# Sums of the down weights made in DRAM, and lower parts of mixer weights split in place: one decoder layer on one core

## The chip, the cores and the metric

The kernel runs on one core of a Trainium2 chip. The core has TensorE (PE, matrix products), VectorE (DVE), ScalarE (ACT), GpSimd (POOL) and SyncE (SP, here a queue that issues transfers); 16 DMA engines move data between DRAM and the on-chip memory (SBUF). The metric is the time of one execution in microseconds (us); lower is better.

## The reference

One layer over 512 tokens of width 1024, in float32:

```python
x = x + 0.5 * rms_norm(swiglu(rms_norm(x, g1), w_gate1, w_up1, w_down1), p1)
x = x + rms_norm(hybrid_mixer(rms_norm(x, g2), w_in, ...), p2)
x = x + 0.5 * rms_norm(swiglu(rms_norm(x, g3), w_gate2, w_up2, w_down2), p3)

def swiglu(h, w_gate, w_up, w_down):          # 1024 -> 2816 -> 1024
    return (silu(h @ w_gate) * (h @ w_up)) @ w_down
```

The mixer projects with `w_in`, runs four heads of differential attention and eight heads of a sparse attention with three branches, and projects back with `w_out`.

## The kernel before

**Two parts of each operand.** TensorE works on float32r, so each float32 operand is split in an upper part (a cast) and a lower part (the value less the upper part). A product takes three matmuls: upper by upper, upper by lower, lower by upper. The function `split` makes both parts: the cast on ACT or DVE (line 404), the subtraction on DVE (line 407). A loaded weight piece is 128 x 1024 float32, 512 KB; it lands in a tile of the pool `raw` (four of them), and its two parts go to the pool `ring` (twelve).

**Seven products in place of eight.** The gate, up and most of the down products are done with the Strassen-Winograd scheme: a 2 x 2 block product with seven block products (numbered 1 to 7) and sums of blocks. For the down weights, `down_products` cuts rows 768 to 2815 of `w_down` in two row halves `kh` and two column halves `jh`; each such block is cut in four quarter rows `q`, so that a piece is again 512 KB. `ORDER` = (1, 5, 6, 2, 7, 4, 3) is the order of the products. Products 1, 2 and 3 take a block as it is. Product 5 takes block (0,0) + block (0,1); product 6 adds block (1,1) to that; product 4 adds block (1,0) to the sum of 6; product 7 takes block (0,1) + block (1,1). `factor` loads the quarters and DVE adds them (line 601), for products 5, 6 and 4 in place in the tiles `ff1du` or `ff2du`, 16 additions in each block. Then `split` makes `ff1dw53h` and `ff1dw53l`: product 5, quarter row 3, upper and lower part. The left operands are `ff1dl`. Line 808 is the matmul of these products. The other 768 rows are done plainly (line 768).

**Lower parts of mixer weights prepared ahead.** For three groups of 512 columns of `w_in` (four pieces each) `ahead` loads a piece during the first feed-forward block (`pre`), casts it on ACT (line 352), subtracts on DVE (line 353) and stores the lower part to DRAM (`low`, line 354). In the mixer `piece` loads the piece anew, makes the upper part (line 377), and loads the lower part from DRAM straight into the ring (line 380, `wp26l` to `wp37l`).

**Norms.** `prenorm` and `postnorm` square on ACT (line 447), and POOL makes the reciprocal root (`rstd`, lines 439 and 440), on which DVE's scaling waits. The normalised tile is transposed on PE and becomes the right operands `xa` (first block), `xb` (mixer), `xc` (second block).

**The order.** Every step is an operation in a graph with a planned cost, its data and its buffers. `Graph.order` plans all engines by list scheduling: the operation with the largest level, the longest path to the end plus a term from the table `BIAS`, goes first as soon as its data and a buffer are there. The program is emitted in that order; each engine then runs its own instructions in that order and waits on semaphores for the others. SP issues nearly all transfers, also in order. A list of edges (`after`) holds back some operations in the plan.

Of the kernel before, what the change touches and what calls it, by code (L numbers as in the profile page):

```python
# [18 lines left out]
P = 128  # L19
# [34 lines left out]
    "ACT:fh>fdl": 5.6, "ACT:fh>fdl@ACT": -68.3, "ACT:fh>fdl@DVE": -0.3, "ACT:fh>fhh": 16.2, "ACT:fh>fhh@DVE": -182,
    "ACT:fhr>fhh": -138.7, "ACT:fhr>fhh@ACT": 20, "ACT:fhr>fhh@DVE": -242.2, "ACT:fp_>fp_": 134.6,
    "ACT:fqu>fqw": 937.3, "ACT:fqv>fqw": 100.3, "ACT:fy>fdp": 44, "ACT:gr>gh": 1255.8, "ACT:htk>hTk": -17.2,
    "ACT:htv>hTv": -173.1, "ACT:k__t>kT": 25.7, "ACT:ls>ls": 40.7, "ACT:n_nm>n_l": 46.2, "ACT:n_t>n_th": 116.1,
    "ACT:n_t>xa": -94.5, "ACT:n_t>xaf0": -210.9, "ACT:n_t>xaf1": 11.9, "ACT:n_t>xb": 327.4, "ACT:n_t>xc": 49.3,
    "ACT:n_t>xcf1": -137.4, "ACT:nc_pc>nc_pc": -84.3, "ACT:nc_t>nc_h": 25.6, "ACT:oN>oTn": 59.7,
    "ACT:oN>oTn@ACT": -12.7, "ACT:oN>oTn@DVE": -5.8, "ACT:pa>cd": 32.4, "ACT:pa>k__dup": 127.2, "ACT:pa>v": -109.4,  # L60
    "ACT:pb>k__dup": 21.1, "ACT:pb>v": 19.9, "ACT:pk>dkd": -48.9, "ACT:pre>pre": 191.7, "ACT:pre>preh": 0.9,
    "ACT:pv>dv": -90.4, "ACT:qTd_>qTd": 7.3, "ACT:qTn_>qTn": -44.2, "ACT:qd>qdd": 5.5, "ACT:qn>qdn": 23.6,
    "ACT:raw>wp": -2.3, "ACT:raw>wp@ACT": 20.1, "ACT:raw>wp@DVE": -4, "ACT:rawff1d>fdwh": 18.3,
    "ACT:rawff1d>fdwh@ACT": -113.1, "ACT:rawff1d>fdwh@DVE": -13.4, "ACT:rawff1q>fqw": 3.5, "ACT:rawff2d>fdwh": -25.9,
    "ACT:rawff2d>fdwh@ACT": -55.9, "ACT:rawff2d>fdwh@DVE": -67.9, "ACT:rawff2q>fqw": -83.9, "ACT:uk>uk": -98.6,
    "ACT:uv>uv": -22.7, "ACT:wrk>wk": 42.2, "ACT:wrv>wv": -96.2, "ACT:xaf0>xa": 12.9, "ACT:xaf0>xa@ACT": -0.2,
    "ACT:xaf0>xa@DVE": -99.7, "ACT:xaf1>xa": 5.7, "ACT:xaf1>xa@ACT": -49.8, "ACT:xaf1>xa@DVE": 21.3,
    "ACT:xcf0>xc": -165.4, "ACT:xcf0>xc@ACT": -92.6, "ACT:xcf1>xc": -156.2, "ACT:xcf1>xc@DVE": 213.5,
    "ACT:xi>n_ss": -6, "ACT:xj>n_ss": -11.3, "ACT:xm>n_ss": 95.1, "ACT:xrv>Xv": 189.3, "ACT:xrv>Xv@ACT": -72.1,
    "ACT:xrv>Xv@DVE": -45, "ACT:z>o_ss": 13.3, "DVE:acc>oN": -6, "DVE:cd_t>kc": 8, "DVE:ck>kcT": -19,  # L70
    "DVE:cmask>cmb": -77, "DVE:cmk>uk": -91.8, "DVE:cmv>uv": 103.6, "DVE:cv>vc": -15, "DVE:d>d_p": -21.7,
    "DVE:d_acc>o": 29.2, "DVE:d_r>d_p": 40.3, "DVE:d_t>d_th": 53.2, "DVE:dkt>dk": 7.8, "DVE:dl>d_r": -29.5,
    "DVE:dl>do_r": -0.4, "DVE:dmask>dmb": 5.2, "DVE:do_rr>o": 39.5, "DVE:do_t>oTd": 3.5, "DVE:fb>fhs": -65.9,
    "DVE:fb>fp_": 8.2, "DVE:fc>fhs": 24.7, "DVE:fc>fp_": 0.5, "DVE:fc__sg>fh": 23.8, "DVE:fd>fhs": -37.7,
    "DVE:fdp>fy": 12, "DVE:fdq>fy": 19.9, "DVE:fdr>fy": 1.9, "DVE:fds>fdl": 1.5, "DVE:fdu>fdwl": 62.2,
    "DVE:fh>fdl": -29.3, "DVE:fh>fds": 14.2, "DVE:fh>fh": 11.2, "DVE:fh>fhl": 92.5, "DVE:fh>fhl@DVE": 9.3,
    "DVE:fh>fhl@POOL": 1.1, "DVE:fhr>fhl": 156.6, "DVE:fp_>fh": 53.9, "DVE:fp_>fhs": 43.6, "DVE:fp_>fp_": 39.7,
    "DVE:fqu>fqw": 1255.3, "DVE:fqv>fqw": -218.6, "DVE:fy>fdr": 4.2, "DVE:gr>gh": 1080.8, "DVE:gsub>gsub": -24.1,
    "DVE:htk>hTk": -33.2, "DVE:htv>hTv": -60.3, "DVE:k__t>kT": 46.9, "DVE:lp>ls": 49, "DVE:ls>nlam": 0.6,
    "DVE:n>n_p": 4.9, "DVE:n_cf>n_p": 22, "DVE:n_cf>n_p@DVE": -1.2, "DVE:n_cf>n_p@POOL": 14, "DVE:n_l>n_cf": -8.8,  # L80
    "DVE:n_t>n_th": -9.5, "DVE:n_t>xa": -96.2, "DVE:n_t>xb": 0.5, "DVE:n_t>xc": 1861.1, "DVE:nc>nc_pc": -160.3,
    "DVE:nc_t>nc_h": -18.1, "DVE:oN>oTn@DVE": 0.7, "DVE:o_yg>xi": 22.6, "DVE:o_yg>xm": -74.8, "DVE:o_yg>xo": 136.3,
    "DVE:pa>k__dup": -42.2, "DVE:pb>k__dup": 6.6, "DVE:pb>v": 5.1, "DVE:pek>xrk": 235.1, "DVE:pev>xrv": 8.5,
# [11 lines left out]
    "PE:dkd>dk": -91, "PE:fdl>fy": 29.8, "PE:fqw>fa": 45.6, "PE:fqw>fb": -9.4, "PE:fqw>fc": 11096.3, "PE:gh>g_": 819,
    "PE:k__dup>kT": -118.5, "PE:n_p>n_th": 301.1, "PE:n_th>acc": 901.3, "PE:n_xn>n_t": 76.4, "PE:n_xn>xb": 123.4,
    "PE:n_xn>xc": -1.5, "PE:nc_h>acc": -5.5, "PE:nc_pc>nc_h": 103.1, "PE:o>oTd": 3.3, "PE:qTd>d_p": 30.9,
    "PE:qTn>n_p": -8.1, "PE:qTn>nc": 92.9, "PE:qdd>qTd": 32.2, "PE:qdn>qTn": -22.2, "PE:uk>hTk": 71.3,
    "PE:uv>hTv": 32.4, "PE:warm>warm": 23.6, "PE:wk>ck": -115.9, "PE:wp>cd": 543, "PE:wp>dkd": -66.7,
# [5 lines left out]
    "SP:g_mix_norm_post>g_mix_norm_post": 1.3, "SP:g_mix_norm_pre>g_mix_norm_pre": 52, "SP:gr>gr": 118.4,
    "SP:lamt>lamt": 110.2, "SP:low>wp": -30.4, "SP:pre>low": -83.8, "SP:pre>pre": 52.2, "SP:raw>raw": -2024,
    "SP:rawff1d>rawff1d": 312.4, "SP:rawff1q>rawff1q": 455.3, "SP:rawff2d>rawff2d": -5.8, "SP:rawff2q>rawff2q": 238.4,
    "SP:trig>trig": 3.2, "SP:wrk>wrk": -5.4, "SP:x>xm": 90.4, "SP:x>xo": -11, "SP:xi>xi": 427.6, "SP:xj>x": -7.4,
    "SP:xj>xj": 6.2, "SP:xm>x": -6.1, "SP:xm>xm": -3.5, "SP:xo>xo": -8.8,
# [1443 lines left out]
```

## Time and profile before

| | |
|---|---|
| median of 3 runs | 1001.36 us (1000.78 to 1003.04) |
| profiled execution | 1003.56 us, of which the span from first to last instruction is 1001.8 us |
| PE, DVE, ACT, POOL busy in the span | 983.5, 882.9, 589.5, 32.3 us |
| granted TensorE clock, mean | 0.995 of full speed (2.4 GHz) |
| moved by the hardware queue | 153.30 MB, 45.4% of 16 DMA engines' span |

A busy engine is one that runs an instruction; waits and the issuing of transfers do not count. The span runs from the first instruction to the last, the time of the execution has a little more around it. The first block's gate and up stage runs to about 242 us, its down stage to 350, the mixer to 658, the second block to the end.

### The profile page before, as it was taken

What the parts mean: (1) busy time and instruction counts of PE and PEld (TensorE: products, weight loads), DVE (VectorE), ACT (ScalarE), POOL (GpSimd) and SP (SyncE); (2) the same over time, 40 slices, a digit from 0 to 9 for tenths busy, and PEclk for the clock granted to TensorE, in tenths of its full rate; (3) what the DMA queues carried; (4) which work ended last, traced back from release to release, by engine and by line L of the source; (5) the groups of instructions that cost most, each with busy time, mean ns of one, the idle gap of its engine ahead of it and who ended that gap; (6) DMA issues with size and microseconds to landing.
All of it is one profiled execution on the core that took longest, in us unless ns stands there. A gap on an engine that the chain in (4) does not pass through costs nothing.

```text
span 1001.8 us, 17153 instructions
## 1 busy us (share of the span) xinstructions
PE 983.5 (98%) x6504; PEld 893.9 (89%) x6504; DVE 882.9 (88%) x1612; ACT 589.5 (59%) x1143; POOL 32.3 (3%) x68
## 2 busy tenths in 40 slices
...
GB/s 336 64 86 179 168 178 127 164 173 242 258 222 293 244 179 147 190 168 1 169 1 110 59 167 86 106 232 53 137 106 135 68 136 43 86 281 244 231 210 84
DMA packets 100420, 154.39 MB, mean 154 GB/s; under 512 B 11121, under 2 KB 61553, under 8 KB 100338
## 3 DMA queue, kind: packets, MB, share of 16 engines
q1 hardware_dynamic: 100338, 153.30, 45.4%
...
## 4 chain that ended last, share of the span: by engine, by line
PE 85%; DVE 6%; DMA 4%; ACT 2%; issue 1%; SPq 0%; POOL 0%; DVEq 0%; POOLq 0%; ACTq 0%
PE ff2b L664 9%; PE ff1b L664 9%; PE ff1y L808 7%; PE ff2c L664 6%; PE ff1c L664 6%; PE ff2a L664 6%; PE ff1a L664 6%; PE ff2y L808 5%; PE z L1410 4%; PE ff2y L768 3%; PE ff1y L768 2%; PE n_t L1306 2%; DMA rawff2d<-ff_w_down 1%; PE n L1190 1%; PE acc L398 1%
## 5 line engine op out<-in xcount | busy, mean ns | idle before, releaser
L1203 ACT ACTIVATE n_p<-n_p,n_nm 128x128 f32<-128x128 f32 (+3 forms) x64 | 35.3, 554 | 9.0 <-DVE n_nm L1201 8.6
L1201 DVE CUSTOM_DVE_ANT_0 n_p<-n,dmb 128x128 f32<-128x128 f32 (+3 forms) x64 | 28.3, 486 | 5.9 <-PE n L1191 5.6
L407 DVE TENSOR_TENSOR n_th<-n_t,n_th 128x512 fp32r<-128x512 f32 x40 | 25.8, 684 | 6.6 <-ACT n_th L404 6.4
L404 ACT CAST n_th<-n_t 128x512 fp32r<-128x512 f32 x40 | 21.6, 594 | 7.0 <-PE n_t L1306 6.7
L439 POOL TENSOR_SCALAR o_ms<-o_ss 128x1 f32<-128x1 f32 x12 | 4.0, 335 | 664.6 <-ACT junk L447 664.5
L691 ACT ACTIVATE ff1p<-ff1p 128x256 f32<-128x256 f32 x30 | 12.5, 418 | 19.2 <-DVE ff1p L703 19.2
L691 ACT ACTIVATE ff2p<-ff2p 128x256 f32<-128x256 f32 x30 | 12.5, 417 | 16.5 <-DVE ff2p L703 15.7
L1203 ACT ACTIVATE d_p<-d_p,d_nm 128x128 f32<-128x128 f32 (+3 forms) x32 | 17.7, 556 | 5.7 <-DVE d_nm L1201 5.5
L1306 PEld LDWEIGHTS n_t<-ident,n_p 128*128 128x128 f32 x160 | 18.6, 140 | 2.5
L1306 PE MATMUL n_t<-ident,n_p 128*128 128x128 f32 x160 | 20.7, 272 | 0.0
L703 DVE TENSOR_TENSOR ff2p<-ff2p,ff2b 128x512 f32<-128x512 f32 x30 | 20.4, 681 | 0.3 <-PE ff2b L664 0.3
L1190 PE MATMUL n<-kT,qTn 128*128 128x128 f32 (+3 forms) x64 | 20.4, 335 | 0.0
L703 DVE TENSOR_TENSOR ff1p<-ff1p,ff1b 128x512 f32<-128x512 f32 x30 | 20.4, 680 | 0.0
L1191 PE MATMUL n<-kT,qTn 128*128 128x128 f32 (+3 forms) x64 | 19.6, 321 | 0.0
L569 DVE TENSOR_TENSOR o_yg<-ff2y,g_ff_norm_post 128x512 f32<-128x512 f32 x8 | 5.5, 689 | 14.3 <-ACT junk L447 14.3
L447 ACT ACTIVATE junk<-ff2y 128x512 bf16<-128x512 f32 x8 | 4.8, 597 | 21.3 <-PE ff2y L768 21.3
L398 PE MATMUL acc<-n_th,v 128*64 128x512 f32 x40 | 16.1, 402 | 0.0
L1201 DVE CUSTOM_DVE_ANT_0 d_p<-d,dmb 128x128 f32<-128x128 f32 (+3 forms) x32 | 14.7, 486 | 1.2 <-PE d L1191 1.2
L399 PE MATMUL acc<-n_th,v 128*128 128x512 f32 x40 | 15.7, 393 | 0.0
L470 PE MATMUL n_t<-ident,n_xn 128*128 128x128 f32 x96 | 13.3, 286 | 1.2 <-DVE n_xn L463 1.2
L703 DVE TENSOR_TENSOR ff2p<-ff2c,ff2p 128x512 f32<-128x512 f32 x20 | 13.8, 688 | 0.3
L1296 DVE TENSOR_SCALAR n_p<-n_p,n_cf 128x128 f32<-128x128 f32 (+3 forms) x42 | 13.8, 380 | 0.3
...
## 6 DMA issues: line engine op xcount, KB each, us to landing
rawff1d<-ff_w_down SPq DMA_DIRECT2D x36, 512.0 KB, 4.7
rawff2d<-ff_w_down SPq DMA_DIRECT2D x36, 512.0 KB, 5.0
rawff1q<-ff_w_gate SPq DMA_DIRECT2D x22, 512.0 KB, 5.8
rawff1q<-ff_w_up SPq DMA_DIRECT2D x22, 512.0 KB, 4.3
rawff2q<-ff_w_gate SPq DMA_DIRECT2D x22, 512.0 KB, 5.1
rawff2q<-ff_w_up SPq DMA_DIRECT2D x22, 512.0 KB, 4.2
raw<-w_in SPq DMA_DIRECT2D x20, 512.0 KB, 4.5
pre<-w_in SPq DMA_DIRECT2D x12, 512.0 KB, 4.2
```

Of the source, the lines that this page charges most:

```text
L398: nc.tensor.matmul(oh, vh, b(1), start=False, stop=False)
L407: V.tensor_sub(lo(), src(), f32(hi()))
L664: nc.tensor.matmul(o, T[k][:, s, i * P:(i + 1) * P], T[xm][:, r, i, :], start=start and e + i + s + r == 0, stop=stop and i == 3 and s == ...
L691: op("ACT", act(256), lambda: A.activation(T[sg][:, :256], T[sg][:, :256], AF.Silu), w=[sg])
L703: op("DVE", dve(512), lambda: fn(T[out], T[x], T[y]), r=[k for k in (x, y) if k != out], w=[out])
L768: nc.tensor.matmul(T[f"{f}y{t}{j}"], T[a[s]][:, sl], wp[i](r)[:, j, :], start=start and s + r == 0, stop=c == rest[-1] and s == 1, skip_gr ...
L808: nc.tensor.matmul(T[ys[u]], T[k][:, s, q % 2 * 2 + n, u * P:(u + 1) * P], T[ws[r]][:, n, :], start=m in (1, 5, 6) and q + n + s + r == 0, ...
L1190: nc.tensor.matmul(T[b][:, :L], qt[:, 0, h, :], k()[:, :L], start=True, stop=False)
L1201: op("DVE", dve(L), lambda: V.tensor_tensor_reduce(T[p][:, :L], T[b][:, :L], T["dmb"][:, S - L:], -1.0, 3e38, ALU.add, ALU.min, T[nm][:, 0 ...
L1203: op("ACT", act(L, 0.22), lambda: A.activation(T[p][:, :L], T[p][:, :L], AF.Exp, bias=T[nm][:, 0:1], scale=-1.0, accum_out=T[l][:, col:col ...
L1306: nc.tensor.transpose(T[bt][:, h * P:(h + 1) * P], T[p[h]][:, kb * P:(kb + 1) * P], ident)
L1410: nc.tensor.matmul(T[y[j]], T[f"oT{t}{'nd'[k < 4]}{s}"][:, k % 4, :], wp[wo[k]](r)[:, j, :], start=k == 4 and s + r == 0, stop=k == 3 and ...
```

## The change

For each block 16 sums of quarters are made in DRAM: SP copies the first summand from the weight tensor to a DRAM tile, then POOL issues a transfer that adds the second summand to it while it moves (accumulation). The sums for products 6 and 4 take an earlier sum from DRAM as the second summand. Each sum is then loaded like any piece, so every `factor` has one load, and the 16 additions of each block on DVE are gone, with the tiles `du`. In the plan these transfers may start after the fifth weight load of the first block, and after the third of the second; POOL's accumulations have an engine of their own in the plan (`DQ`), with a cost of 11.0 and a latency of 1.0. The three groups of `w_in` no longer have lower parts prepared ahead: they are split where they are used, as the other pieces are. The table `BIAS` has new values and more entries, and terms with an engine (`@PE`) now count for operations that have one engine only; the first norm has two names, `na` and `nb`, so that its tiles 0 and 1 can have other terms than 2 and 3. The order of the whole program is planned anew.

```diff
@@ BIAS (some 200 lines, values and entries)
-    "DVE:n_t>xa": -96.2, "DVE:n_t>xb": 0.5, "DVE:n_t>xc": 1861.1, "DVE:nc>nc_pc": -160.3,
+    "DVE:n_t>xa": -96.2, "DVE:n_t>xb": -141.8, "DVE:n_t>xb@DVE": -3267.4,
...
@@ Graph
-    LAT = {"PE": 0.28, "ACT": 0.18, "DVE": 0.2, "POOL": 0.2, "SP": 2.0}
+    LAT = {"PE": 0.28, "ACT": 0.18, "DVE": 0.2, "POOL": 0.2, "SP": 2.0, "DQ": 1.0}
...
-                    heapq.heappush(ready[e], (-o.level - (BIAS.get(f"{kind_of(o)}@{e}", 0.0) if len(o.eng) > 1 else 0.0), o.n, o))
+                    heapq.heappush(ready[e], (-o.level - BIAS.get(f"{kind_of(o)}@{e}", 0.0), o.n, o))
...
@@ down_products, factor
-    def down_products(f):
+    def down_products(f, after):
...
-        def add(dst, a, b, r):
-            op("DVE", dve(1024), lambda: V.tensor_add(T[dst], T[a], T[b]), r=[k for k in r if k != dst], w=[dst], port=True, chain="sum")
+        def src(q, kh, jh):
+            r0 = (2 * SPILL + 8 * kh + 2 * q) * P
+            return io[f"{f}_w_down"][0, r0:r0 + 2 * P, jh * 512:(jh + 1) * 512].rearrange("(k p) b -> p k b", p=P)
+        sums = {}
         for q in range(4):
-            new(f"{f}du{q}", ("M", "m_u"), [P, 1024])
+            for m, a, b in ((5, (0, 0), (0, 1)), (6, (1, 1), 5), (7, (0, 1), (1, 1)), (4, (1, 0), 6)):
+                k = f"{f}sum{m}{q}"
+                d = sums[m, q] = dram.tile([P, 2, 512], F32, name=k)
+                more, r = (sums[b, q], [f"{f}sum{b}{q}"]) if isinstance(b, int) else (src(q, *b), [])
+                op("SP", 1.46, lambda d=d, a=src(q, *a): nc.sync.dma_start(d, a), w=[k], after=after)
+                op("DQ", 11.0, lambda d=d, more=more: nc.gpsimd.dma_start(d, more, accum_op=ALU.add, max_dma_last_dim=4096), r=r, w=[k], after=after, chain="acc")
...
-    def factor(f, m, raw, add):
+    def factor(f, m, sums, src):
         for q in range(4):
...
+            u = new(f"raw{f}d{m}{q}", "raw", [P, 1024])
+            part = {1: (0, 0), 2: (1, 0), 3: (1, 1)}.get(m)
+            a, r = (src(q, *part), []) if part else (sums[m, q], [f"{f}sum{m}{q}"])
+            v = lambda u=u: T[u].rearrange("p (a b) -> p a b", a=2)
+            pdma.append(op("SP", 1.46, lambda v=v, a=a: nc.sync.dma_start(v(), a), r=r, w=[u], chain="dma"))
@@ layer
-    dp1 = down_products("ff1")
+    dram = ctx.enter_context(tc.tile_pool(name="dram", bufs=1, space=bass.MemoryType.DRAM))
+    dp1 = down_products("ff1", [qdma[4]])
...
-        prenorm("n1", t, g1, "xa", "xi", True)
+        n1 = "na" if t < 2 else "nb"
+        prenorm(n1, t, g1, "xa", "xi", True)
...
-    low_i = {c: [ahead(*in_rows(c, 512, j)) for j in range(4)] for c in (512, 0, 1024)}
+    low_i = {c: (None,) * 4 for c in (512, 0, 1024)}
...
-    dp2 = down_products("ff2")
+    dp2 = down_products("ff2", [qdma[46]])
```

## Rows read from the trace of the kernel before

**Rows 1.** The page: span, and busy time of TensorE.

```profile
span 1001.8 us, 17153 instructions
...
PE 983.5 (98%) x6504; PEld 893.9 (89%) x6504; DVE 882.9 (88%) x1612; ACT 589.5 (59%) x1143; POOL 32.3 (3%) x68
```

**Rows 2.** Busy us: PE, PEld, DVE, ACT, POOL; then clock, DMA share, GB/s.

```profile
0.00:25.00 25.00, 20.83 (x129) 18.13 (x130) 18.03 (x33) 20.50 (x42) 4.13 (x14) 1.00 0.95 336
```

**Rows 3.** Busy time by engine in stretches of the stages; columns as above.

```profile
25.00:225.00 200.00, 199.16 (x1661) 198.93 (x1660) 192.16 (x326) 114.97 (x204) 0.00 (x0) 1.00 0.45 143
225.00:262.00 37.00, 36.95 (x234) 33.31 (x232) 35.58 (x44) 16.12 (x25) 0.00 (x0) 1.00 0.72 247
262.00:275.00 13.00, 8.84 (x26) 6.82 (x27) 12.39 (x12) 8.09 (x10) 0.00 (x0) 0.74 0.72 247
335.00:425.00 90.00, 88.25 (x497) 76.11 (x496) 70.48 (x135) 50.93 (x107) 8.66 (x18) 1.00 0.55 187
425.00:575.00 150.00, 149.82 (x873) 123.49 (x871) 115.70 (x353) 109.91 (x258) 0.00 (x0) 1.00 0.24 85
910.00:950.00 40.00, 39.57 (x174) 32.03 (x173) 38.09 (x39) 20.74 (x23) 0.00 (x0) 1.00 0.68 222
```

**Rows 4.** Waits of TensorE: total us, times, longest us.

```profile
PE ff1y L808 <- ACT ff1dw53h L404: 2.4, 1, 2.4
PE ff1y L808 <- DVE ff1dw53l L407: 1.8, 1, 1.8
...
PE pa L389 <- DVE wp8l L407: 0.6, 1, 0.6
PE ff2c L664 <- DVE xc L407: 0.3, 1, 0.3
```

**Rows 5.** Busy time by engine in one window of 2 us.

```profile
266.00:268.00 2.00, 1.33 (x3) 1.14 (x4) 2.00 (x3) 1.12 (x2) 0.00 (x0) 0.50 0.93 349
```

**Rows 6.** DVE's busy time at line 601 alone; clock, DMA share, GB/s.

```profile
0.00:262.00 262.00, 3.67 (x4) 1.00 0.54 176
0.00:1001.80 1001.80, 38.66 (x32) 1.00 0.46 154
```

**Rows 7.** DVE's busy time at line 353 alone.

```profile
0.00:262.00 262.00, 10.97 (x9) 1.00 0.54 176
0.00:1001.80 1001.80, 14.63 (x12) 1.00 0.46 154
```

**Rows 8.** ScalarE's busy time at line 352 alone.

```profile
0.00:1001.80 1001.80, 12.57 (x12) 1.00 0.46 154
```

**Rows 9.** The timeline around the wait: start, us, what.

```profile
261.99 1.22 DVE L601 TENSOR_TENSOR ff1du<-rawff1d,rawff1d 128x1024 f32<-128x1024 f32 x1
263.12 2.35 DVE L601 TENSOR_TENSOR ff1du<-ff1du,rawff1d 128x1024 f32<-128x1024 f32 x2
```

**Rows 10.** Transfers: the hardware queue, and issues with KB each, us to landing.

```profile
q1 hardware_dynamic: 100338, 153.30, 45.4%
...
rawff1d<-ff_w_down SPq DMA_DIRECT2D x36, 512.0 KB, 4.7
```

**Rows 11.** The timeline of SP's queue: start, us, what it issues.

```profile
29.03 24.98 SPq L332 DMA_DIRECT2D rawff1q<-ff_w_up  x2
...
252.59 0.88 SPq L332 DMA_DIRECT2D rawff1d<-ff_w_down  x2
...
602.45 1.98 SPq L332 DMA_DIRECT2D rawff2q<-ff_w_up  x2
...
894.06 0.88 SPq L332 DMA_DIRECT2D rawff2d<-ff_w_down  x2
```

**Rows 12.** The timeline of POOL.

```profile
348.40 0.30 POOL L439 TENSOR_SCALAR o_ms<-o_ss 128x1 f32<-128x1 f32 x1 [329.42 <-ACT junk L447]
...
663.21 0.59 POOL L439 TENSOR_SCALAR n_ms<-n_ss 128x1 f32<-128x1 f32 x1 [2.86 <-ACT junk L447]
```

**Rows 13.** DVE's and ACT's busy time at line 404 alone.

```profile
25.00:262.00 237.00, 1.38 (x2) 17.14 (x24) 1.00 0.49 159
```

More of the change, by code (lines that the diff above doesn't have):

```diff
@@ L54 @@
[L54 to L83, printed above, removed]
@@ L95 @@
[L95 to L99, printed above, removed]
@@ L105 @@
[L105 to L109, printed above, removed]
+    "ACT:acc>ol": -15.1, "ACT:cd_t>kc@ACT": 453.3, "ACT:ck>kcT": 75.7, "ACT:cmv>prev": -52.6,
@@ new lines @@
+    "ACT:xi>nb_ss": -6, "ACT:xj>n_ss": 31.3, "ACT:xj>na_ss": -11.3, "ACT:xj>nb_ss": -11.3, "ACT:xm>n_ss": 95.1,
+    "ACT:xm>na_ss": 95.1, "ACT:xm>nb_ss": 95.1, "ACT:xrv>Xv": 210.6, "ACT:xrv>Xv@ACT": -13128.4,
+    "ACT:xrv>Xv@DVE": 755.2, "ACT:z>o_ss": 13.3, "ACT:z>o_ss@ACT": -6926.2, "DVE:cd_t>kc": -359.2,
+    "DVE:cd_t>kc@DVE": 1197.3, "DVE:ck>kcT": 136.3, "DVE:cmask>cmb": -77, "DVE:cmask>gates": -560.9,
+    "DVE:cmask>gates@DVE": -2397.2, "DVE:cmk>uk": -95.2, "DVE:cmv>uv": -230.8, "DVE:cv>vc": -15,
@@ new lines @@
+    "DVE:fdp>fdr": 11.9, "DVE:fdp>fy": -226.2, "DVE:fdq>fy": 66.8, "DVE:fdr>fy": 1.9, "DVE:fds>fdl": 1.5,
+    "DVE:fdu>fdwl": 62.2, "DVE:fh>fdl": -29.3, "DVE:fh>fds": 123.1, "DVE:fh>fh": 11.2, "DVE:fh>fhl": 92.5,
+    "DVE:fh>fhl@DVE": 9.3, "DVE:fh>fhl@POOL": 1.1, "DVE:fhr>fhl": 253.2, "DVE:fp_>fh": 53.9, "DVE:fp_>fhs": -77.5,
+    "DVE:fp_>fhs@DVE": 14.7, "DVE:fp_>fp_": 39.9, "DVE:fp_>fp_@DVE": 6004.4, "DVE:fqu>fqw": 1801.4,
+    "DVE:fqu>fqw@DVE": 34598.8, "DVE:fy>o_yg": -0.2, "DVE:gates>nc_pc": -4.8, "DVE:gr>gh": 3378.5,
@@ new lines @@
+    "DVE:gr>gh@DVE": 136036, "DVE:gsub>gsub": 1.2, "DVE:htk>hTk": -33.2, "DVE:k__t>kT": 46.9,
+    "DVE:lamt>lp@DVE": 175.6, "DVE:lp>ls": 49, "DVE:ls>nlam": 0.6, "DVE:ls>nlam@DVE": -23018.4, "DVE:n>n_p": 4.9,
+    "DVE:n>na_p": 4.9, "DVE:n>nb_p": 4.9, "DVE:n_cf>n_p": -70.4, "DVE:n_cf>n_p@DVE": -1.2, "DVE:n_cf>n_p@POOL": 14,
+    "DVE:n_l>n_cf": -8.8, "DVE:n_t>n_th": -9.5, "DVE:n_t>xa": -96.2, "DVE:n_t>xb": -141.8, "DVE:n_t>xb@DVE": -3267.4,
+    "DVE:n_t>xc": 2428.3, "DVE:na_cf>na_p": 22, "DVE:na_cf>na_p@DVE": -1.2, "DVE:na_cf>na_p@POOL": 14,
@@ new lines @@
+    "DVE:na_l>na_cf": -8.8, "DVE:na_t>na_th": -9.5, "DVE:na_t>xa": -94.1, "DVE:na_t>xa@DVE": -138.5,
+    "DVE:na_t>xb": 0.5, "DVE:na_t>xc": 1861.1, "DVE:nb_cf>nb_p": 22, "DVE:nb_cf>nb_p@DVE": -1.2,
+    "DVE:nb_cf>nb_p@POOL": 14, "DVE:nb_l>nb_cf": -8.8, "DVE:nb_t>nb_th": -9.5, "DVE:nb_t>xa": -85.1,
+    "DVE:nb_t>xa@DVE": 24709.9, "DVE:nb_t>xb": 0.5, "DVE:nb_t>xc": 1861.1, "DVE:nc>nc_pc": -160.3,
+    "DVE:nc_t>nc_h": -22.9, "DVE:oN>oTn": -4.8, "DVE:oN>oTn@DVE": 0.7, "DVE:o_yg>xi": 22.6, "DVE:o_yg>xm": -35.9,
@@ new lines @@
+    "DVE:xi>na_xn@DVE": -91.8, "DVE:xi>nb_xn": 24.9, "DVE:xi>nb_xn@DVE": 453.6, "DVE:xj>n_xn": 616.7,
+    "DVE:xj>na_xn": 201.8, "DVE:xj>nb_xn": 201.8, "DVE:xm>n_xn": 74.1, "DVE:xm>na_xn": 31.3, "DVE:xm>nb_xn": 31.3,
+    "DVE:xrk>Xk": -49, "DVE:xrk>Xk@DVE": 51.4, "DVE:xrk>Xk@POOL": -0.9, "DVE:xrv>Xv": 89.8, "DVE:xrv>Xv@DVE": 124.3,
+    "DVE:xrv>Xv@POOL": -18.4, "DVE:z>o_yg": 50.7, "DVE:z>o_yg@DVE": -35734.9, "PE:cd>kc": 12.3, "PE:cd>kc@PE": 142,
+    "PE:d_p>o": 12.8, "PE:d_th>d_acc": -4, "PE:fdl>fy": 29.8, "PE:fqw>fa": 48.1, "PE:fqw>fa@PE": 2047.1,
@@ new lines @@
+    "PE:wp>fc__": 3.9, "PE:wp>fy": 139.2, "PE:wp>fy@PE": -4899.8, "PE:wp>pb": 25.5, "PE:wp>pv": 0.5,
+    "PE:wp>pv@PE": -44.6, "PE:wp>qdd": 16.8, "PE:wp>qdn": 654.9, "PE:wp>uk": 153.6, "PE:wp>uv": 103.8,
+    "PE:wp>uv@PE": 19701.5, "PE:wp>z": 19.2, "PE:wv>cv": -75.8, "POOL:Xv>Xv": -59.3, "POOL:do_ss>do_r": -120.6,
+    "POOL:n_ss>n_r": 664.9, "POOL:n_ss>n_r@POOL": 5646.4, "POOL:na_ss>na_r": 2357.1, "POOL:na_ss>na_r@POOL": 66051.7,
+    "POOL:nb_ss>nb_r": 665.9, "POOL:o_ss>o_r": 62.9, "SP:cmask>cmask": 183.7, "SP:dmask>dmask": -75.7,
@@ L110 @@
+    "SP:xj>xj@SP": -1566.5, "SP:xm>x": -6.1, "SP:xm>xm": -3.5, "SP:xo>xo": 86.1,
 }
@@ L245, in order @@
                             for p in self.tiles[k][0]:
-                                heapq.heappush(back, (o.end + self.LAT[e] * (e != "SP"), p, k))
+                                heapq.heappush(back, (o.end + self.LAT[e] * (e not in ("SP", "DQ")), p, k))
                     for y, data in o.outs:
-                        lat = 0.0 if y.eng == (e,) and e != "SP" else self.LAT[e]
+                        lat = 0.0 if y.eng == (e,) and e not in ("SP", "DQ") else self.LAT[e]
                         y.at = max(y.at, o.end + lat if data else o.start + 1e-6)
@@ L630, in factor @@
             h, l = (new(f"{f}dw{m}{q}{x}", "ring", [P, 2, 512], F32R) for x in "hl")
-            split(lambda u=u: T[u].rearrange("p (a b) -> p a b", a=2), lambda h=h: T[h], lambda l=l: T[l], 1024, [u], [h], [l],
-                  chain="ring", sbuf=True)
+            split(v, lambda h=h: T[h], lambda l=l: T[l], 1024, [u], [h], [l], chain="ring", sbuf=True)
     def ffn(f, xT, down, after, seven=False):
```

95 lines of the change are left out of this document (57 added, 38 removed), and 23 rows, old and new, of the table BIAS.

## The prediction

> **What bounds the kernel now.** I read the page's first parts, then the stretches by engine, then who TensorE (PE) waited for, then single lines. PE is busy 983.5 of 1001.8 us [rows 1], so at most 18.3 us of idle can come back, plus what a lowered clock cost. In the first 25 us PE is idle 25 - 20.83 = 4.17 us, while x and the first weights arrive [rows 2]; the change does not touch that directly. In the gate and up stage of the first feed-forward block PE is busy 199.16 of 200 us and VectorE (DVE) 192.16: two engines nearly full, PE the bound [rows 3]. One place stands out: in the 13 us from 262, PE is busy 8.84 us, idle 4.16, and the granted clock is 0.74 on average. Before that, from 225, DVE is busy 35.58 of 37 us, and with 12.39 of 13 it has no gap there either [rows 3]. In the list of waits the two longest PE waits are at line 808, for the upper and the lower part of `ff1dw53`, 2.4 and 1.8 us: 4.2 us [rows 4]. It is the piece of the down weights for product 5, last quarter row, and its input is a sum of quarters made on DVE.
>
> The clock makes that wait dearer. In the 2 us from 266 it is 0.50 of full speed [rows 5]: 2.4 GHz fell to 1.2 GHz after PE had stood still, and it came back after PE had worked again. A mean of 0.74 over 13 us [rows 3] means (1 - 0.74) x 13 / 0.5 = 6.8 us at half speed; some 1 us of that lies inside the wait (in the window at 266 PE works 1.33 of 2 us), so (6.8 - 1.0) / 2 = 2.9 us of work was lost. The stall costs 4.2 + 2.9 = 7.1 us in all. The rest of the idle time is spread: 1.75 us from 335 to 425, 0.43 from 910 to 950 and 0.18 from 425 to 575 [rows 3], and the end, where the last tiles are normalised.
>
> **The change, part by part.** *Sums removed from DVE.* Line 601 makes 32 additions, 38.66 us, 16 in each block; 3.67 us of them lie before 262 [rows 6]. They go. *Lower parts not prepared.* Line 353 makes 12 subtractions, 14.63 us, of which 10.97 before 262 [rows 7]; ScalarE's twelve casts at line 352 are 12.57 us [rows 8]. The casts go for good, since the mixer already makes the upper part from its own copy; the subtractions move into the mixer, to where the weights are used. Between 225 and the end of the wait DVE so loses the 3.67 us of sums before 262 and 1.22 + 2.35 us for three more behind them [rows 9], 7.2 us, beside the subtractions of that stretch, where PE was late by 4.2. The transfers are off DVE, and the pieces are ready first. I take the whole stall away: -7.1 us. At 910 to 950 the same sums delay the second block; the idle 0.43 us goes too, and I take -0.4.
>
> *Transfers.* The page's queue moved 153.30 MB in 45.4% of the span [rows 10]; that is 454.8 us, or 1.56 us of all DMA engines for 512 KB. Out go 16 loads for sums (72 become 56) and 36 transfers for the lower parts (12 in, 12 out, 12 back): 52, or 81 us. In come 32 copies and 32 accumulations in DRAM. A copy reads and writes, 1.6 to 3.1 us; an accumulation reads two and writes one, for which no row exists. Its bounds: 1.6 us if it passes like one load, 14.1 us if it takes three landings of 4.7 us [rows 10] one after the other. I take 5 (three passes). For the first block that is 16 x (3.1 + 5) = 130 us less the load and the store of each of nine subtractions before 262 [rows 7], 18 transfers or 28 us: about 102 us, into the 55% of 200 us that the DMA engines have free in 25 to 225 [rows 3], 110 us. It fits, hardly; loads have slack, since SP's own queue stood for 24.98 us over two loads at 29 us, with no tile free for the second [rows 11]. Price: nothing, at worst the ring of prepared weights gets shorter.
>
> *When the sums are wanted.* The new load of a sum waits on SP, which issues in order; behind it all later weight loads stand. The last load for product 5 is issued at about 253, and at 895 in the second block [rows 11]. The copies can begin about 29 and 604 (after SP's lines at those times), and the sum for product 5, quarter row 3, is the 13th of 16. So each accumulation may take (253 - 29) / 13 = 17 us in the first block and (895 - 604) / 13 = 22 in the second. Both are above my upper bound of 14.1, so I take 0. The Trainium skill, DMA: Bandwidth & Descriptors, section Anatomy of one DMA, fits 2.0 us plus bytes over 436 GB/s for such a transfer; with three passes of 512 KB its estimate would be 5.6 us, and the sum would be the same.
>
> *POOL.* It now issues the accumulations, each after its copy has landed and some after an earlier sum has. Behind them in its queue stand the reciprocal roots of the norms. For 329.42 us before 348.40 POOL has none [rows 12], so the first block is free of that. The second block's sums start near 604, and there such roots stand too, the last from 663.21 on [rows 12]. What follows that root is PE's product at 672, which already waits 0.3 us for it through `xc` [rows 4]. Bounds: 0 to 14.1 us, if one accumulation stands just ahead and waits a whole one; a gap like the 2.86 us ahead of that last root hides part [rows 12]. I take +0.5.
>
> *The mixer.* 14.6 us of subtractions come into 425 to 575, where DVE is busy 115.7 of 150 [rows 3]; 34.3 us free cover them. Below nothing is possible too: reloads of lower parts no longer stand in SP's queue. Without cover it is at most +14.6. The nearest row is a lower part that is made in place already, `wp8l`, for which PE waits 0.6 us once [rows 4], in a stretch with many such pieces. I take +1.0. From 335 to 425 the removed transfers let `w_in` come sooner: 0 to -1.75, taken -0.6.
>
> *The order.* All priorities and the whole order are computed anew, with more terms. No row shows an order that hasn't run. I take 0; bounds are -4 (most of the start's 4.17 us, or as much in the mixer) and +4.
>
> Sum: -7.1 - 0.4 + 0.5 + 1.0 - 0.6 = -6.6 us. The profiled execution took 1003.56 us, 1.76 around its span of 1001.8; the sum makes a span of 995.2, and 996.96 for that execution. The median of the three runs is 1001.36, 2.2 below the profiled one; so I predict 994.8.
>
> **The rivals.** *A: the roots wait behind an accumulation (slower).* POOL stands with a waiting accumulation at 659 to 664; the last root comes D late and PE idles D at 672, with 2.9 us more for the clock as at 265. Against 6.6 gained it is slower than before by 2 us from D = 5.7; at D = 9 it gives 994.8 + 9 + 2.9 = 1006.7. For it: the 0.3 us wait shows a chain without slack [rows 4]. Against: 16 accumulations are spread over 290 us. The Trainium skill (DMA: Bandwidth & Descriptors, section Two DMAs through the same engine are not ordered) says that the issuing engine has to wait for the first transfer's completion; no row of before shows POOL doing so. Chance 0.09.
>
> *B: sums come late because POOL can't prepare transfers beside a busy DVE (slower).* If POOL works on them only while DVE is idle, it has 200 - 192.16 = 7.84 us in 200 [rows 3]; 16 of the size of its 0.59 us instruction [rows 12] need 9.4 us. The missing 1.6 us takes 1.6 / 0.039 = 41 us: 994.8 + 41 = 1036. Deciding from 0.49 us each. The Trainium skill, SBUF — State Buffer, section SBUF: two separate sides, has the milder rule that a VectorE copy in a two-port mode locks descriptor writing out. DVE's casts at line 404 are two in 25 to 262, 1.38 us [rows 13]; by that rule the sums lose 1.4 us of 224 and nothing changes. Chance 0.06.
>
> *C: the mixer takes back what the stall gave (no change).* Half of the moved 14.6 us shows at PE: +7.3 instead of +1.0: 1001.1. DVE's 34 free us speak against it. Chance 0.10.
>
> *D: the stall only gets shorter*, since product 5 waits for SP or for another DVE step: 3 of 7.1 gained, 998.9. Chance 0.08.
>
> *E: the new order also closes idle time at the start and in the mixer:* 994.8 - 5 = 989.8. Chance 0.17.
>
> **The numbers.** The likeliest, the stall gone and the rest even, has 0.50, and its own range is 992 to 998. About 2 us (0.2%) is what a measurement can tell from no change. Faster: 0.50 + 0.17 + 0.08 = 0.75; same: 0.10; slower: 0.09 + 0.06 = 0.15. The range reaches from E, 988, to the lesser half of A, 1004; B, the worse of A and an order still better than E are left out, less than 0.2.
>
> **What would show it.** Right: no PE wait at line 808 over 0.5 us, clock 1.00 from 225 to 335, DVE busy some 39 us less over the span and ScalarE 12 less, 56 loads `rawff*d`. POOL: accumulations all landed before 240 and 880. Wrong: PE waits for `DMA rawff*d` with SP waiting for a sum (sums late); an idle PE at 660 to 675 with POOL behind a transfer (A); PE idle in 425 to 575 for `wp26l` to `wp37l` (C).

## The result, and the profile after

The changed kernel takes 1028.1 us (median; 1024.9 to 1032.7), the kernel before 1001.4: the ratio is 1.027, 95% interval 1.020 to 1.033. The forecast was 994.8. The profiled execution is the slowest of the three, 1032.7 us. The first lines of its page answer to [rows 1], the queues to [rows 10]; q0 is the queue of the accumulations.

```profile
span 1030.9 us, 17190 instructions
...
PE 988.9 (96%) x6504; PEld 900.6 (87%) x6504; DVE 848.9 (82%) x1576; ACT 577.8 (56%) x1135; POOL 66.7 (6%) x100
...
q1 hardware_dynamic: 93874, 142.81, 41.9%
q0 software_dynamic: 6656, 16.78, 9.5%
```

DVE lost 34 us of work and ScalarE (ACT) 11.7, where 39 and 12 were forecast, and TensorE (PE) is no less busy; the span still grew by 29.1 us. (POOL's busy time here counts its issuing of accumulations.) 9.5% of the span over 32 accumulations is 3.06 us of all DMA engines for one. Where the time went is seen best by stages. Each stage ends at a product that every version has, so this table can be read across plans: "gate 1" runs from the start to the first `ff1y` product, "down 1" to the last one, "mixer" to the first gate product of the second block, "gate 2" to the first `ff2y` product, "down 2" to the last, "end" to the end of the span (starts of matmuls in each trace, us).

```
                            gate 1  down 1  mixer  gate 2  down 2  end   span
before                       242.7   121.2  294.9   226.7   109.8  6.5  1001.8
after                        268.9   113.1  305.9   227.6   108.6  6.9  1030.9
difference                   +26.2    -8.1  +11.0    +0.9    -1.2  +0.4   +29.1
```

The forecast gain came: 9.3 us less in the two down stages. The wait at `ff1dw53` is gone; its products run in one row at full clock (first and last start of eight):

```profile
L841 PE MATMUL ff1y<-ff1dw53h,ff1dl x8: 389/389/389, 287.9 to 290.4; 128*128 128x512 f32 x8
```

The loss is in gate 1, and in the mixer. These stretches of gate 1 answer to [rows 3]: busy us of PE, PEld, DVE, ACT, POOL, then clock, DMA share, GB/s.

```profile
25.00:50.00 25.00, 24.46 (x205) 24.21 (x204) 24.93 (x43) 16.37 (x31) 3.20 (x3) 1.00 0.97 298
50.00:75.00 25.00, 25.00 (x211) 25.00 (x210) 19.85 (x35) 11.09 (x21) 3.79 (x4) 1.00 1.04 269
75.00:100.00 25.00, 16.05 (x114) 15.88 (x113) 14.73 (x26) 7.81 (x17) 3.81 (x4) 0.80 0.98 213
100.00:125.00 25.00, 22.75 (x188) 22.37 (x187) 17.00 (x30) 9.15 (x18) 4.65 (x5) 1.00 0.99 195
125.00:150.00 25.00, 15.03 (x114) 15.06 (x115) 19.71 (x37) 10.13 (x20) 0.00 (x0) 0.80 0.62 211
```

The DMA engines are full from 25 to 125, where before the mean over 25 to 225 was 0.45 [rows 3], and PE stands twice, about 79 to 88 and 123 to 135, with the granted clock down to 0.50 of full speed behind each stop. The waits from 50 to 150 (total, times, longest) say for what:

```profile
DVE ff1q31u L568 <- DMA rawff1q<-ff_w_up: 13.3, 1, 13.3
PE ff1b L697 <- ACT ff1q50w L587: 11.7, 1, 11.7
PE ff1b L697 <- DVE ff1p L736: 8.9, 1, 8.9
...
DVE lp L972 <- DMA lamt<-lambda_k: 5.8, 1, 5.8
DVE cmb L962 <- DMA cmask<-cmask: 5.7, 1, 5.7
```

PE's two longest waits make 20.6 us; the lowered clock makes most of the rest of the 26.2. PE waits for DVE and ACT, and these wait for transfers. DVE takes its work in order: it stood 13.3 us for one gate load, and later for two small loads (`cmask`, `lamt`) that only the mixer wants, with the gate weights' parts queued behind. SP's queue answers to [rows 11], POOL's to [rows 12] (start, us, what it issues):

```profile
30.02 35.29 SPq L647 DMA_DIRECT2D ff1sum<-ff_w_down  x15
65.41 2.29 SPq L375 DMA_DIRECT2D rawff1q<-ff_w_up  x1
```

```profile
44.96 0.84 POOL L648 DMA_DIRECT2D ff1sum<-ff1sum  x1 [13.30 <-DMA ff1sum<-ff_w_down]
...
117.73 0.84 POOL L648 DMA_DIRECT2D ff1sum<-ff1sum  x1 [3.70 <-DMA ff1sum<-ff1sum]
```

The plan issues 15 copies in a row at 30, and all 16 accumulations by 118, though the first sum is loaded at 261. The signs that the prediction named for being right came (no wait at the down products, clock 1.00 from 225 to 335, 56 loads `rawff*d`, DVE's saving but for 5 us), and none of those for being wrong: no sign watched gate 1.

### The profile page after: what moved, and what is told of

Same layout as the page of the kernel before. It is cut to its first block, busy times and chain, and to the rows that moved or that the text cites. A ratio compares the mean times of both kernels' runs of the same rounds, so it can differ in the third digit from the quotient of the medians.

```text
span 1030.9 us, 17190 instructions
## 1 busy us (share of the span) xinstructions
PE 988.9 (96%) x6504; PEld 900.6 (87%) x6504; DVE 848.9 (82%) x1576; ACT 577.8 (56%) x1135; POOL 66.7 (6%) x100
## 5 line engine op out<-in xcount | busy, mean ns | idle before, releaser
L1237 ACT ACTIVATE n_p<-n_p,n_nm 128x128 f32<-128x128 f32 (+3 forms) x64 | 35.3, 553 | 10.7 <-DVE n_nm L1235 10.7
L697 PE MATMUL ff1b<-xa,ff1q40w 128*128 128x256 f32 x36 | 6.1, 331 | 11.7 <-ACT ff1q50w L587 11.7
L697 PEld LDWEIGHTS ff1b<-xa,ff1q40w 128*128 128x128 f32 x36 | 5.7, 237 | 11.9 <-issue 11.9
L1332 ACT ACTIVATE n_p<-n_p,n_cf 128x128 f32<-128x128 f32 (+3 forms) x29 | 14.3, 537 | 1.2 <-DVE n_cf L1322 1.2
```

What stands on the lines that cost most here:

```text
L697: nc.tensor.matmul(o, T[k][:, s, i * P:(i + 1) * P], T[xm][:, r, i, :], start=start and e + i + s + r == 0, stop=stop and i == 3 and s == ...
L1237: op("ACT", act(L, 0.22), lambda: A.activation(T[p][:, :L], T[p][:, :L], AF.Exp, bias=T[nm][:, 0:1], scale=-1.0, accum_out=T[l][:, col:col ...
```

## The experiments

The theories, as the expectations name them. **T1**: the copies stand in a row on SP and hold up the quad loads behind them; **T4** is T1 with SP's queue alone as the cause. **T2**: what the transfers take of the DMA engines costs, wherever they stand. **T3**: the new order and its biases are worse by themselves. **T5**, formed after the first four runs: the engine time of the sums costs only where it is bunched beside a load that DVE or PE stands for. **T6**: the read of what is added to makes an accumulation dear. **T7**: the missing lower parts cost the mixer. Stages of all runs, as in the table above:

```
                            gate 1  down 1  mixer  gate 2  down 2  end   span   ratio to before (95%)
1 paced                      251.2   113.1  300.8   237.0   108.6  6.9  1017.6  1.013 (1.010 to 1.016)
2 first copies by POOL       256.1   113.1  304.3   228.5   108.6  6.8  1017.4  1.015 (1.011 to 1.018)
3 copies alone               242.3   113.1  300.7   226.4   108.6  6.8   997.9  0.997 (0.995 to 0.999)
4 sums on DVE                242.5   114.8  301.9   226.5   115.0  6.8  1007.5  1.003 (1.001 to 1.005)
5 paced and parted           242.8   113.1  302.2   230.4   108.6  6.9  1004.0  1.000 (0.999 to 1.002)
6 before + sums in DRAM      253.5   113.1  295.2   230.0   108.6  6.6  1006.9  1.006 (1.004 to 1.008)
7 plain copies               254.0   113.1  299.1   226.8   108.6  6.8  1008.5  1.008 (1.006 to 1.010)
8 accumulations moved        270.3   113.1  302.0   229.3   108.6  6.9  1030.1  1.020 (1.018 to 1.022)
9 lower parts back           251.9   113.1  294.7   230.9   108.6  6.6  1005.8  1.007 (1.005 to 1.008)
10 before, first block       250.4   113.1  295.4   226.7   109.6  6.6  1001.8  1.000 (0.999 to 1.001)
11 before, both, spread      250.5   113.1  295.3   226.7   108.6  6.6  1000.8  1.000 (0.998 to 1.001)
12 before, both, 10 + 6      243.9   113.1  295.5   226.7   108.6  6.6   994.4  0.992 (0.991 to 0.994)
13 before, both, 9 + 7       242.8   113.1  295.1   226.7   108.6  6.6   992.9  0.992 (0.991 to 0.993)
```

The ratios are of medians over several executions. The stages are of one profiled execution each, which took 7.8 us more than the median in run 8 and at most 3.6 us more in the other runs (4.6 in the changed kernel); a difference of a few us between two rows needs a wait or a lowered clock to go with it.

**Run 1, paced.** The planned order is kept; only the 64 new transfers are taken out and put in elsewhere (`pairs` holds each sum's copy and accumulation; two lines that change nothing are left out where the dots stand):

```diff
     order = g.order()
+    for i, (c, a) in enumerate(pairs):
...
+        n = (6 + 2 * (i % 16), 50 + 2 * (i % 16))[i // 16]
+        for o, at in ((c, n), (a, n + 2)):
+            order.remove(o)
+            order.insert(order.index(qdma[at]) + 1, o)
```

> The changed kernel, with every copy and every accumulation taken out of its place in the written order and put behind a quad load of the gate stage: copy i of the first block behind quad load 6 + 2i, of the second behind quad load 6 + 2i as well, its accumulation two quad loads later; nothing else moves on any engine. T1 (the copies are issued 15 in a row and stop the quad loads behind them on SP's queue and on the DMA engines): the losses at 75 to 150 (25.6 us) and at 600 to 725 (some 11.5) go and the gain at the down products stays, 1028.1 - 37.1 = 991 us; 988 to 1000. T2 (what the transfers take of the DMA engines in all is too much, wherever they stand): the loss is spread, not gone, 1015 to 1030. T3 (the planned order and its new biases are worse by themselves): 1015 to 1030, with the losses on PE where they were.

1015.8 us: outside T1's range, and just inside those of T2 and T3. The stages fit none of the three as it was put: gate 1 gave back 17.7 of its 26.2 us, gate 2 lost 9.4 more. One large stop was left in each block, and the waits name them (85 to 130, then 590 to 720):

```profile
DVE cmb L962 <- DMA cmask<-cmask: 4.5, 1, 4.5
DVE lp L972 <- DMA lamt<-lambda_k: 4.4, 1, 4.4
...
POOL ff2sum L648 <- DMA ff2sum<-ff_w_down: 25.2, 4, 10.0
...
DVE n_xn L506 <- POOL n_r L483: 8.8, 3, 7.9
...
PE n_t L513 <- DVE n_xn L506: 8.5, 1, 8.5
```

In the first block DVE still stands for the mixer's small loads. In the second, POOL waits with an accumulation for its copy, and a root of the norms stands behind it: rival A, at its place and nearly its size, made by my own spacing. My 11.5 us for the second block was also put to the wrong account: run 4 shows that 7 of them have nothing to do with transfers.

**Run 2, first copies by POOL.** (`lambda ...` shortens its arguments.)

```diff
-op("SP", 1.46, lambda ...: nc.sync.dma_start(d, a), w=[k], after=after)
+op("SP", 1.46, lambda ...: (nc.gpsimd if f == "ff1" else nc.sync).dma_start(d, a), w=[k], after=after)
```

> The changed kernel, with the 16 copies of the first block alone issued by POOL instead of SP, in the same place of the order (SP's queue then holds only quad loads there); the second block is as it was. T4, a form of T1 in which SP's queue alone matters: quad loads go out on time, the 25.6 us at 75 to 150 go, about 1003 us (1000 to 1008). T1 in the form that the DMA engines are what is full (share 0.97 to 1.04 from 25 to 125): the quad loads are issued early but land late, and most of the loss stays, 1015 to 1030.

1018.4 us, in the range of full engines and outside T4's; gate 1 at 256.1 keeps half of its loss. With SP free PE is busy 25.00 of 25 from 75 to 100, so the first stop needs the row on SP's queue; the second, at 100 to 125 (15.48 of 25), stays with the engines at 0.92. T4 holds for one of the two stops, and run 3 shows that the row alone makes neither. The edit moves the accumulations too: POOL issues the copies first, and the last accumulation goes out at 140.9 instead of 117.7.

**Run 3, copies alone.** The line that makes the accumulations is left out.

> The changed kernel without the 32 accumulations: the sums stay copies of their first quarter (so the second summands are left out of the computation), and the 32 copies are where they were. T1: the copies still stand 15 in a row before the quad loads, but the DMA engines have 16 x 3.06 = 49 us less to do per block: part of both losses stays, 1005 to 1018. T2 in the form that the accumulations are what costs: both losses go, 990 to 997. T3: 1015 to 1030.

999.9 us, below T1's range and 2.9 us above that of T2's form, in which the accumulations are what costs: gate 1 takes 242.3 us with the same 15 copies in a row on SP, and what is left of the loss lies in the mixer. The copies alone do no harm, and SP's queue shows why:

```profile
29.04 18.54 SPq L647 DMA_DIRECT2D ff1sum<-ff_w_down  x15
54.77 0.37 SPq L375 DMA_DIRECT2D rawff1q<-ff_w_up  x1
```

Before, SP stood from 29 to 54 with no tile free for the next quad load [rows 11]. A row of 18.5 us fits into that stand, and the next quad load goes out at 54.8, where before it went out just ahead of 54. Beside accumulations the same row takes 35.3 us, and that load goes out at 65.4.

**Run 4, sums on DVE.** `down_products`, `factor` and the cap `m_u` of the kernel before, everything else of the changed one.

> The changed kernel with its new biases, its rule that a bias holds on a single engine too, and without the prepared lower parts, but with the sums of the down weights made by DVE in SBUF as before. T1 (the losses come with the transfers): near the kernel before, 995 to 1006 us, the stall at the down products back, DMA shares in 25 to 125 as before. T3 (the order is worse by itself): above 1010.

1006.0 us, T1's range. Gate 1 and gate 2 are as before, so their losses come with the transfers; but the mixer takes 301.9 us, 7 more than before, without one sum in DRAM, which speaks for T3 there (run 9 will tell otherwise). One thing expected did not come: the stall in the first block's down stage is not back. PE has no gap where it had one before [rows 3]:

```profile
262.00:275.00 13.00, 13.00 (x59) 10.74 (x59) 13.00 (x13) 6.97 (x7) 0.00 (x0) 1.00 0.77 254
```

So 6.4 of the 8.1 us in down 1 come also with DVE's sums kept, from the new order and the preparation that is gone. In the second block the new order with DVE's sums is 5.2 us slower than before (115.0).

**Run 5, paced and parted.** As run 1, with

```diff
-        n = (6 + 2 * (i % 16), 50 + 2 * (i % 16))[i // 16]
+        n = ([6, 8, 10, 12, 14, 16, 26, 28, 29, 31, 32, 34, 35, 37, 38, 40][i % 16],
+             [60, 62, 63, 65, 66, 68, 69, 71, 72, 74, 75, 77, 78, 80, 81, 83][i % 16])[i // 16]
```

> Like the paced kernel, with the places chosen by what its two stalls showed: in the first block six sums stand before the small loads of the mixer (behind quad loads 6 to 16) and ten after them (26 to 40), none beside them; in the second all 16 stand behind quad loads 16 to 39, so that no accumulation is in front of a root on POOL. T5 (an accumulation costs nothing where no load is due that DVE stands for and no root is behind it on POOL): the stalls at 100 to 125 and at 675 to 690 of the paced kernel (some 7 and 8 us with the fall of the clock) go, 994 to 1003. T2 (what they take of the DMA engines costs wherever they stand): a loss stays or moves, 1010 to 1020.

1003.5 us, half a us above T5's range; gate 1 is 242.8. All 32 accumulations are made, by the same engines, and the 26 us are gone: T2 falls, T5 stands for gate 1. Gate 2 keeps 3.7 us, and the mixer its 7.

**Run 6, before + sums in DRAM.** Old biases, lower parts prepared; transfers in the places of run 5.

> The kernel before, old biases and prepared lower parts kept, with the sums in DRAM as its only edit and their copies and accumulations in the places of the run beside it. T5 with the gain that the copies alone showed (some 6 us against the sums on DVE): 992 to 999. If the prepared lower parts (loads and stores at 100 to 240) fill the engines that the sums need: 1002 to 1015.

1008.8 us: the second expectation. The mixer is back at 295.2 and down 1 is at 113.1, but gate 1 takes 253.5, beside the loads and stores of the lower parts.

**Run 7, plain copies.**

```diff
-... nc.gpsimd.dma_start(d, more, accum_op=ALU.add, max_dma_last_dim=4096) ...
+... nc.gpsimd.dma_start(d, more, max_dma_last_dim=4096) ...
```

> The changed kernel with each accumulation made a plain copy of the same bytes in the same place on POOL (the second summand takes the place of the first, so the sums are left out of the computation). T6 (it is the read of what is added to that costs: 3.06 us of all engines for an accumulation, some 1.5 for a copy issued by POOL): half of the engines' load goes, and most of the loss, 1000 to 1010. If it is POOL's transfers as such: 1020 to 1030.

1011.2 us, 1.2 above T6's range and below the other. The places in the order and the bytes asked for are the same, the engines' time is half:

```profile
q0 software_dynamic: 4608, 16.78, 4.9%
```

4.9% of 1008.5 us over 32 is 1.54 us for one, against 3.06. Gate 1 loses 11.3 us instead of 26.2; without any (run 3) it loses nothing. The stretch from 30 to 118 of the changed kernel, of this run, and of run 3:

```profile
30.00:118.00 88.00, 78.36 (x629) 78.02 (x630) 69.56 (x120) 40.70 (x78) 14.88 (x16) 0.94 1.00 247
```

```profile
30.00:118.00 88.00, 80.85 (x671) 80.30 (x669) 74.78 (x132) 42.60 (x82) 9.57 (x16) 0.98 0.87 285
```

```profile
30.00:118.00 88.00, 88.00 (x736) 88.00 (x734) 84.84 (x149) 48.73 (x90) 0.00 (x0) 1.00 0.63 198
```

Run 3's share 0.63 and 16 x 3.06 us in 88 (0.56) would be 1.19: more than there is, so the accumulations can't fit beside the other transfers. Over these 88 us run 7's copies would fit, 0.63 + 16 x 1.54 / 88 = 0.91. But in the shorter stretch from 30 to 75, where run 3 has a share of 0.73, nine of them come to 0.73 + 9 x 1.54 / 45 = 1.04, and the engines are full there. Full engines do no harm by themselves, though: in run 3 they are full from 30 to 60, and PE and DVE go on. These two stretches, run 7's first:

```profile
30.00:75.00 45.00, 45.00 (x378) 45.00 (x377) 39.85 (x69) 23.89 (x45) 5.45 (x9) 1.00 1.00 333
```

```profile
30.00:60.00 30.00, 30.00 (x252) 30.00 (x251) 29.90 (x51) 19.14 (x37) 0.00 (x0) 1.00 1.00 334
```

In these three kernels engines that are full for 30 us cost gate 1 nothing, for 45 us 11.3 and for 88 us 26.2. T6 holds for the price of one accumulation; that it is the read of what is added to was not told apart from other work of the addition.

**Run 8, accumulations moved.** The copies left in their row, the accumulations alone put behind the later quad loads in the written order.

> The changed kernel with its copies left in their row of 15 and 16, and the accumulations alone put in the places of the paced and parted kernel (the first six of the first block a few quad loads later). T5: the copies without accumulations cost nothing, so this is as fast as that kernel, 994 to 1004. T1 (the row of copies on SP's queue is what costs): 1010 to 1025.

1024.1 us, T1's range, and gate 1 at 270.3: nothing gained there. That does not make T1 right. The expectation stood on a wrong premise. A place in the written order holds an instruction back only behind others of its own engine, and POOL has none in the first block; the accumulations that it makes from earlier sums start where those of the changed kernel did, 45.0 to 117.7 there (first and last start):

```profile
L648 POOL DMA_DIRECT2D ff1sum<-ff1sum x8: 829/838/847, 43.2 to 118.5; - x8
```

It is the copies, on SP's ordered queue, that let the sums begin. The last copy of the row is issued at 62; behind it the accumulations follow one another, as each sum for product 6 or 4 waits for an earlier one. In the second block, where POOL has other work, the move took hold: the accumulations start at 693 instead of 633, and the mixer takes 302.0 us instead of 305.9.

**Run 9, lower parts back.** Run 5 with the line `low_i = {c: [ahead(...) ...] ...}` of before.

> The paced and parted kernel (new biases, sums in DRAM) with the lower parts of the mixer weights prepared again, as in the kernel before. It asks where the 7 us go that the stage from the last down product to the first gate product of the second block takes more in every kernel with the new biases (294.9 us before, 300.7 to 302.2 in the runs with the copies alone, with the sums on DVE, and with the sums parted). T7 (the missing lower parts cost it): that stage comes back to 294 to 297, while the first gate stage rises from 242.8 towards 250 (their loads and stores meet the sums): 1000 to 1010 in all. T3 in its small form (the new order costs it): the stage stays at 300 to 303: 1003 to 1015.

1008.1 us, as T7 expected. The mixer falls from 302.2 to 294.7 with the new biases kept, and gate 1 rises from 242.8 to 251.9. PE's longest waits from 365 to 670 in run 5 and from 370 to 660 in this one:

```profile
PE d L1224 <- DVE oT0d L450: 1.6, 1, 1.6
PE do_t L1427 <- DVE qTd L450: 1.1, 1, 1.1
PE d L1224 <- DVE d_nm L1235: 1.0, 1, 1.0
```

```profile
PE z L1444 <- DVE oT0d L450: 1.4, 1, 1.4
PE qn L432 <- DVE wp24l L450: 0.4, 1, 0.4
```

In run 5 DVE makes the 12 lower parts (`wp26l` to `wp37l`) at 431 to 533, and no wait is for one of them: the waits of `d` and `do_t` come behind, from 540 on. The whole mixer stage before, in run 5 and in run 7:

```profile
363.90:658.80 294.90, 292.97 (x1701) 247.72 (x1699) 245.03 (x670) 209.46 (x514) 17.38 (x30) 1.00 0.33 113
```

```profile
355.90:658.10 302.20, 297.04 (x1699) 251.46 (x1698) 256.32 (x675) 210.05 (x517) 19.96 (x30) 0.98 0.28 88
```

```profile
367.10:666.20 299.10, 293.89 (x1700) 248.22 (x1700) 254.91 (x674) 209.79 (x517) 23.48 (x35) 1.00 0.39 125
```

PE idles 1.9 us before, 5.2 in run 5 and 5.2 in run 7. So of the 7 us some 3 are waits; most of the rest is the clock, which falls in run 5 (0.98 in the mean) and not in run 7, whose mixer is 3.1 us shorter. Whether the waits come from DVE's time or from the order that the planner makes around these subtractions was not told apart.

**Runs 10 and 11, before with a wider spread.** Run 6's kernel, with the second block's sums on DVE (10) or in DRAM (11), the first block's behind quad loads 6, 8, 10 to 13, 14, 14, 17, 26, 29, 33, 37, 41, 43, 43. In both the last sum of the first block, and in run 11 that of the second too, adds one that is not yet complete; this changes values, and what it does to the waits was not measured by itself.

> The kernel before with the sums of the first block alone in DRAM (old biases and prepared lower parts kept; the second block's sums on DVE), the copies spread further: eight behind quad loads 6 to 14, one behind 17, seven from 26 to the last, so that they stand in the free stretches of SP's queue and no two follow each other after 100 us. T5: first gate stage 243 to 247, down products 113, the rest as before: 993 to 998. If what the sums take of the engines costs beside the lower parts even so: 1000 to 1006.

> The same with the sums of both blocks in DRAM, the second block's spread over quad loads 16 to 43. T5: the second gate stage costs at most 1 us more than before (3.3 in the run with them closer together) and the second down stage 1.2 less, 993 to 998; else 998 to 1006.

1003.0 and 1002.2 us, the second expectation of both: no change. Gate 2 is cured (226.7) and the second block's sums give their 1.2 us; gate 1 stays at 250.5, with its stop now at 200 to 235, where three sums stand in a row (run 11):

```profile
200.00:225.00 25.00, 22.56 (x189) 22.38 (x188) 18.05 (x29) 11.84 (x20) 2.71 (x3) 1.00 0.98 278
```

**Runs 12 and 13, no row left.** As run 11, the first block's places being 6, 8, 10 to 13, 14, 14, 15, 17, 26, 29, 32, 35, 38, 41 (12) or 6, 8, 10 to 13, 14, 14, 17, 26, 28, 30, 33, 35, 37, 40 (13), and each sum made behind those that it adds (so these runs differ from run 11 in that order too).

> The kernel before (old biases, lower parts prepared) with the sums of both blocks in DRAM, spread once more: ten copies of the first block before the small loads of the mixer (behind quad loads 6 to 17), six after them (behind 26, 29, 32, 35, 38, 41), none at the stage's end, where the run before it lost 4 us at 200 to 235 to three sums in a row; the second block as there. T5: the first gate stage falls from 250.5 to 243 to 247 with the other stages as they were, 993 to 998 us. If the sums and the lower parts can't both be had in the first gate stage: it stays at 249 to 254, 999 to 1005.

> The same with nine sums before the small loads and seven after them, closer together (behind quad loads 26, 28, 30, 33, 35, 37, 40), so that the last one is made some 15 us earlier. T5 by spacing: between the run with ten in that stretch (253.5 for the first gate stage) and the one beside this (243 to 247): 246 to 250, 997 to 1002.

995.0 and 994.5 us: 0.8% faster than before (the intervals end at 0.994 and 0.993), and 3.3% than the change as made. Run 12 is as T5 expected, run 13 better. That run 13 comes out at the forecast of 994.8 is chance: it is another kernel, which keeps the old biases and the prepared lower parts. Its gate 1, from 25 to 225:

```profile
25.00:225.00 200.00, 199.16 (x1660) 198.93 (x1660) 192.03 (x326) 114.01 (x204) 14.08 (x15) 1.00 0.81 227
```

PE's 199.16 us are those of before [rows 3], with the DMA share at 0.81 instead of 0.45: 72 us of transfers more, and PE loses nothing by them.

## Why the prediction was wrong

**The stall at the down products**: right in size. -7.1 and -0.4 were said, -8.1 and -1.2 came. The cause is half right. Taking the sums off DVE is enough (run 6 does only that in the old order, and down 1 is 113.1), but in the first block it isn't needed: with DVE's sums in the new order, run 4, down 1 is 114.8. In the second block it is: there run 4 takes 115.0 us instead of 108.6.

**Transfers, "Price: nothing"**: the step that failed. Its sizes were on the safe side: 5 us for an accumulation, where it takes 3.06; 3.1 for a copy, where it takes 1.7 (in run 3 the hardware queue holds 44.0% of 997.9 us, in run 4 40.7% of 1007.5, 29.0 us less; run 3 has 32 copies more and 16 loads of 1.56 us less: (29.0 + 25.0) / 32). So 76 us a block, not 130, and 110 were free. The room was there, and run 13 uses it. What failed is that the sum spread the load evenly over 25 to 225. The diff says `after=[qdma[4]]`, nothing in it holds a copy back, and 16 accumulations of 3.06 us into the stretch from 30 to 118 don't fit. The price that was put at nothing is 26.2 us in gate 1. The same paragraph's "loads have slack", read from SP's 24.98 us stand at 29 [rows 11], was true, and the slack was these 25 us: the copies alone, 18.5 us, fit into it (run 3), the same copies beside accumulations, 35.3 us, don't. The second stop, at the small loads, lies where the engines were still full (0.99 from 100 to 125). Hidden work has to be checked against the stretch in which it will run, not against the stage.

**When the sums are wanted**: right, and beside the point. Landings of 10.4 and 8.4 us (medians, 30 to 118) lie under the bound of 14.1 and the 17 allowed; the last accumulation went out at 117.7 and the first sum was fetched at 260.9, and that was the trouble. The Trainium skill, DMA: Bandwidth & Descriptors, section Anatomy of one DMA, has a fixed part and bytes over a rate, which made 5.6 us for three passes; the landings measured here, on full engines, are longer.

**POOL**: +0.5 was said. In the changed kernel's own order DVE waits 0.9 us in all for the last norm's roots, so rival A did not happen; run 1 shows that another order brings it, 8.5 us of wait at PE. Rival B is refuted: from 25 to 50 POOL works 3.20 us on accumulations beside a DVE that is idle 0.07 of 25, and no accumulation takes it more than 1.4.

**The mixer**: +1.0 less 0.6 was said, +7.0 came (run 4), and run 9 puts it to the missing lower parts: some 3 us of waits, most of the rest a lowered clock. Rival C had this size, 7.3, at 0.10; but not its signature, a PE wait at the parts themselves. The other 4 us of the mixer's 11 come with the second block's row of copies and accumulations (302.2 in run 5, 302.0 in run 8, 305.9 in the changed kernel): a stop of PE at 672 to 676, behind DVE, which stood 7.9 us for a quad load.

**The order**: 0 was said. Run 9 has the new biases, and its mixer is that of before; with the sums in DRAM no run shows them costing anything by themselves. With DVE's sums they go with 5.2 us more in down 2 (run 4).

So the 29.1 us are 26 for the bunch in gate 1, 4 for that in the second block and 7 for the lower parts, less 9.3 for the down stages, and 1.3 for gate 2 and the end.
